# A two-layer decoder trunk on one core: the output product reads sums that the DMA queues have added up, with four smaller edits in the attention layers

## The chip, the cores and the metric

The kernel runs on one core of a Trainium2 chip. The metric is the device time of one execution in microseconds (us), as the median of several runs. The core's engines work side by side, each on its own instructions in their written order: TensorE (PE) multiplies matrices, VectorE (DVE) and ScalarE (ACT) do elementwise work, GpSimd (POOL) a little of it, and SyncE (SP) issues most of the DMA transfers. POOL can issue DMAs too, from a queue of its own. An engine that waits for one instruction waits with everything behind it.

## The reference, cut to what matters

Two layers on a sequence of 1024 rows of 1024 elements, all in float32. Each layer has an attention, a residual with LayerNorm, a gated feed-forward (ff) and another residual with LayerNorm.

```python
ALPHA = (2 * DEPTH) ** 0.25
for i in range(2):
    y = diff_attention(h, ...) if i == 0 else forgetting_attention(h, ...)
    h = layer_norm(ALPHA * h + y, ln1_g[i], ln1_b[i])
    f = conv_ffn(h, ...)
    h = layer_norm(ALPHA * h + f, ln2_g[i], ln2_b[i])

def conv_ffn(x, w_in, conv_w, conv_b, w_out):       # D_FF = 2816
    gate, up = split(x @ w_in, 2)
    gate = causal_conv_width_3(gate, conv_w) + conv_b
    return (silu(gate) * up) @ w_out
```

The differential attention of layer 0 has 8 pairs of heads. For a pair, one softmax minus lambda times another multiplies the values, and each 128-wide row of the result `o` is divided by its root mean square (`rms_norm`). The forgetting attention of layer 1 has 16 heads; a forget gate per head and row (`f_logit = x @ w_f`, 16 columns) adds a running sum to the scores.

## The kernel before

**Precision.** A float32 operand is kept as two float32r parts, `hi` (a rounded copy, made on ACT, line 89) and `lo` (the rest, a subtraction on DVE, line 91). This is `split`. A product is three matmuls, `mm3` (lines 100 to 102): hi by hi, lo by hi, hi by lo, all added up in one PSUM bank. A plain float32 matmul is shown as two passes (x2 in the timeline).

**Order of the work.** Layer 0's attention, its output projection and norm, its ff up product, its ff output product, and then the same for layer 1. In the attention, the tiles of the next pair's projections (`m<-xh,wh`) fill PE between the scores, the transposes (line 1371) and the value products. Jobs are Python generators. `tick` starts the work of a job and `tock` ends it, and what is written earlier in these functions stands earlier in each engine's queue. Tiles come from named pools with a fixed number of buffers, and an engine waits where the pool has no free one. The framework's scheduler decides the last detail of the order from this.

**Places that the change touches.**
- `scores` (lines 519 to 535): a strip of scores of ln = 128 (qt+1) columns is cut at 512; each part is one matmul with the hi part of the keys (line 533) and one with the lo part (line 534). For ln = 640 the parts have 512 and 128 columns. This happens 32 times, 16 in each layer.
- `diff_values` (lines 597 to 613): the block norm of layer 0. A matmul of all ones with the squares gives every partition the sum over the 128 (line 606, plain float32), and ACT and DVE turn it into the norm's factor. Each of the 8 pairs has two groups of 512 query rows (the last pair three groups).
- `gate_logits` (lines 618 to 636): the forget gates' logits, by `mm3` with 16-wide weights, for 8 blocks of the contraction and 2 halves of the rows, so 48 matmuls.
- `Values.evacuate` (called in `tick`, line 787): copies transposed probabilities out of PSUM as their hi and lo parts, `pt<-m`.
- `gated` (lines 1115 to 1134): for each of the 22 blocks f of the ff's inner dimension, the convolution, silu and two multiplies; the tile is stored to DRAM, `ad[f]`.
- `down_steps` (lines 1144 to 1326): the output product, (1024 x 2816) by (2816 x 1024), by one level of a Strassen-Winograd scheme: 7 products m of quarter operands in place of 8. Each has k = 0..10 blocks of the contraction and j = 0..3 blocks of rows, three matmuls each, so one step (m, k) is 12 matmuls of 512 columns. The passes are ((1,2), (6,5), (7,3), (4,)). For each k, `load_a` and `load_b` fetch quarters of the left operand (from `ad`) and of the weight, `sub` (line 1198) forms the scheme's sums and differences on DVE, `make` splits them into `oa` and `wo`, and `drain` (line 1267) adds a finished bank to the accumulator `acc`. `when(i, ...)` ties a load or a sum to a step, LEAD = 10 steps before its use. `Ffn.run` calls the makes up to AHEAD = 6 steps in advance.
- `Norm` (`stats`, `root`, `apply`, lines 1476 to 1515) for the LayerNorm. In the last pass (m = 4) each row block j is drained, normed and, in layer 1, stored.

Of the kernel before, what the change touches and what calls it, by code (L numbers as in the profile page):

```python
# [48 lines left out]
S2, S3 = 1, 1  # L49
M7, G4 = 15, 5  # L50
# [6 lines left out]
class Trunk:  # L57
# [64 lines left out]
    def consts(self):  # L122
# [14 lines left out]
        self.ones = cp.tile([P, P], F32, name="ones")  # L137
        nc.vector.memset(self.ones, 1.0)
# [381 lines left out]
    def scores(self, q, kd, kl, h, qt, l):  # L520
# [76 lines left out]
    def diff_values(self, of, ob, q0, q1):  # L597
# [3 lines left out]
        rd = self.tp.tile([P, 512], F32, tag="sq", name=self.nm("sq"), bufs=1)[:, :w]  # L601
        nc.scalar.activation(rd, osl, AF.Square)
# [3 lines left out]
        nc.tensor.matmul(ms, self.ones, rd, start=True, stop=True)  # L606
# [3 lines left out]
        nc.vector.scalar_tensor_tensor(ms, ms, P * RMS_EPS, rd, op0=ALU.add, op1=ALU.mult)  # L610
        nc.vector.scalar_tensor_tensor(osl, osl, self.gsub, rd, op0=ALU.mult, op1=ALU.mult)
        nc.vector.tensor_tensor(ms, ms, rd, op=ALU.mult)
# [5 lines left out]
    def gate_logits(self, c):  # L618
        nc = self.nc
        if c == 0:  # L620
            st = self.tmp()[:, :P]
            nc.sync.dma_start(st, self.i["wf"])
            self.wf = [self.cp.tile([P, 128], F32R, name=f"wf{j}") for j in range(2)]
            self.split(*self.wf, st)
# [7 lines left out]
        for kt in range(KT):  # L632
            ws = slice(16 * kt, 16 * kt + 16)
            self.mm3(ps[:16], self.wf[0][:, ws], self.wf[1][:, ws], self.xh[kt, c], self.xl[kt, c],
                     kt == 0, kt == KT - 1)
        nc.vector.tensor_scalar(self.z[:16, c * 512:c * 512 + 512], ps[:16], self.bf, None, op0=ALU.add)

    def forget_gates(self):
# [19 lines left out]
        nc.vector.tensor_tensor_scan(c, self.ones, l, 0.0, op0=ALU.mult, op1=ALU.add)  # L658
# [118 lines left out]
    def tick(self, live, values, job):  # L777
# [8 lines left out]
        for v in values:  # L786
            v.evacuate()
# [18 lines left out]
    def tock(self, values):  # L806

        n = 1 if values and values[0].l == 0 else 2
        for v in values:
            n -= v.turn(n)  # L810
        for v in values:
# [303 lines left out]
    def gated(self, l, f, d):  # L1115
# [16 lines left out]
        nc.vector.tensor_tensor(t[:, :512], t[:, :512], d["b"][:, 512:], op=ALU.mult)  # L1132
        nc.vector.tensor_tensor(t[:, 512:], t[:, 512:], d["b"][:, :512], op=ALU.mult)
        nc.sync.dma_start(self.ad[f], t)

# [8 lines left out]
    def down_steps(self, l):  # L1144
# [3 lines left out]
        self.norm2 = None  # L1148
# [15 lines left out]
        def load_a(k, *blocks):  # L1164

            nonlocal n_h
            for r in blocks:
                if r == 22 or (r, k) == (21, H - 1):
                    if n_h % 2 == 0:
                        self.half = self.qp.tile([P, 1024], F32, tag=f"q{1 - self.own}", name=self.nm("ha"))  # L1170
# [417 lines left out]
```

## Time and profile before

| | |
|---|---|
| median of 3 runs | 2470.56 us (2469.18 to 2472.64) |
| profiled execution | 2472.59 us, of it the span 2470.8 us |
| granted TensorE clock | 0.994 of full speed |
| PE busy | 2421.0 us (98%), 11377 matmuls |
| DVE busy | 1893.9 us (77%) |
| ACT busy | 1239.2 us (50%) |
| POOL busy | 141.2 us (6%) |
| DMA | 266.02 MB, mean 108 GB/s |

The profile shows one execution. A group of instructions gives the busy time, the mean duration and the idle time that stood ahead of it with what ended that idle time. Matmuls are pipelined, and the end of each is modelled, so a row of 0.39 us and the next row's start overlap: what one matmul costs is the distance between two starts. A bracket behind a row of a timeline is the idle time before it and its releaser.

The stages in the span: layer 0's attention to about 443 us, its projection and norm to 590, the up product to 988, the output product to 1160, layer 1's projections and gates to 1275, its attention to 1700, and its second output product from about 2240 to 2460.

### The profile page before, as it was taken

Reading aid. Unit: us, or ns where it says so; the run is one execution under the profiler, and the core shown is the slowest. Engines: PE = TensorE matmul, PEld = TensorE weight load, DVE = VectorE, ACT = ScalarE, POOL = GpSimd, SP = SyncE. Lnnn points to the kernel's source line nnn. Section 1 sums busy time; section 2 is a strip of 40 time slices with the busy share of each in tenths; the row PEclk is TensorE's granted clock in tenths of the full one; section 3 lists DMA queues with packets and bytes.
Section 4 is the critical chain, followed back from the end, with each engine's and each line's share of the span. In section 5 each row is a group of like instructions: output and inputs, shape, how many; then the busy total and the mean of one; then the engine's idle time right before and its main releaser. Section 6 shows DMA issues by size and latency. Waiting matters only on the chain. (4 is left out here: it accounts for less than half of the span.)

```text
span 2470.8 us, 32550 instructions
## 1 busy us (share of the span) xinstructions
PE 2421.0 (98%) x11377; PEld 1984.9 (80%) x11377; DVE 1893.9 (77%) x3588; ACT 1239.2 (50%) x2311; POOL 141.2 (6%) x323
## 2 busy tenths in 40 slices
PE   9999999999999999989999999999999999999998
PEld 7887778778888888878778888888878888888776
DVE  5887877989767667696857777778888666666978
ACT  4555556556544444434545555555465444445344
POOL 2111111010000000000100000000010000000000
PEclk9999999999999999999999999999999999999999
DMA  6223223532322224842422222224223222228622
GB/s 182 65 84 91 81 82 92 174 110 80 103 77 77 95 85 140 298 157 74 138 70 73 65 65 65 65 81 155 94 79 101 77 89 90 77 85 301 206 86 98
DMA packets 111940, 266.02 MB, mean 108 GB/s; under 512 B 17648, under 2 KB 24816, under 8 KB 111776
## 3 DMA queue, kind: packets, MB, share of 16 engines
q1 hardware_dynamic: 110816, 262.83, 33.4%
q8 instruction: 90, 1.47, 0.2%
q0 software_dynamic: 672, 1.05, 0.2%
q14 instruction: 74, 0.61, 0.1%
q10 hardware_dynamic: 288, 0.07, 0.0%
HBM read 182.68 MB, written 47.64 MB: 93 GB/s over the span
## 5 line engine op out<-in xcount | busy, mean ns | idle before, releaser
L100 PE MATMUL m<-xh,wh 128*128 128x512 f32 x768 | 320.3, 417 | 7.0 <-DVE pt L91 6.6
L101 PE MATMUL m<-xl,wh 128*128 128x512 f32 x768 | 302.7, 394 | 1.7 <-DVE xl L91 1.7
L102 PE MATMUL m<-xh,wl 128*128 128x512 f32 x768 | 302.8, 395 | 0.0
L100 PE MATMUL m<-xh,wo 128*128 128x512 f32 x656 | 255.4, 389 | 0.0
L102 PE MATMUL m<-xh,wo 128*128 128x512 f32 x656 | 255.3, 389 | 0.0
L101 PE MATMUL m<-xl,wo 128*128 128x512 f32 x656 | 255.2, 389 | 0.0
L89 ACT ACTIVATE pt<-m 128x512 fp32r<-128x512 f32 (+3 forms) x285 | 137.6, 492 | 182.8 <-PE m L1371 120.6
L540 DVE CUSTOM_DVE_ANT_0 s<-s,mask 128x384 f32<-128x384 f32 (+7 forms) x256 | 194.5, 760 | 42.4 <-PE s L534 41.5
L89 ACT ACTIVATE wo<-wg 128x512 fp32r<-128x512 f32 x168 | 106.5, 634 | 225.0 <-PE m L102 218.4
L100 PE MATMUL m<-q,wo 128*128 128x512 f32 x472 | 184.1, 390 | 0.0
L91 DVE TENSOR_TENSOR pt<-m,pt 128x512 fp32r<-128x512 f32 (+3 forms) x285 | 156.7, 558 | 35.6 <-ACT pt L89 31.7
L101 PE MATMUL m<-q,wo 128*128 128x512 f32 x472 | 183.8, 389 | 0.0
L102 PE MATMUL m<-q,wo 128*128 128x512 f32 x472 | 183.7, 389 | 0.0
L100 PEld LDWEIGHTS m<-xh,wh 128*128 128x128 f32 x768 | 145.7, 190 | 38.3 <-DVE pt L91 11.2
L102 PEld LDWEIGHTS m<-xh,wl 128*128 128x128 f32 x768 | 145.0, 189 | 31.3 <-DVE wl L91 0.2
L101 PEld LDWEIGHTS m<-xl,wh 128*128 128x128 f32 x768 | 145.5, 190 | 27.5 <-issue 2.9
L89 ACT ACTIVATE wo<-t 128x512 fp32r<-128x512 f32 x132 | 82.8, 627 | 145.3 <-PE m L102 133.2
L91 DVE TENSOR_TENSOR wo<-wg,wo 128x512 fp32r<-128x512 f32 x168 | 115.3, 687 | 41.1 <-ACT wo L89 40.2
L527 POOL CAST qz<-q 64x128 fp32r<-64x128 f32 x256 | 96.6, 378 | 845.1 <-PE s L534 773.2
L100 PEld LDWEIGHTS m<-xh,wo 128*128 128x128 f32 x656 | 123.1, 188 | 26.0 <-ACT pt L1093 0.6
L101 PEld LDWEIGHTS m<-xl,wo 128*128 128x128 f32 x656 | 123.1, 188 | 25.7
L102 PEld LDWEIGHTS m<-xh,wo 128*128 128x128 f32 x656 | 123.1, 188 | 25.6 <-DVE wo L91 0.2
(341 smaller groups left out, 5875.6 us busy)
## 6 DMA issues: line engine op xcount, KB each, us to landing
wst<-in_w SPq DMA_DIRECT2D x46, 512.0 KB, 3.9
t<-in_wi SPq DMA_DIRECT2D x44, 512.0 KB, 4.5
ad<-t SPq DMA_DIRECT2D x44, 512.0 KB, 3.7
ha<-ad SPq DMA_DIRECT2D x88, 256.0 KB, 5.5
wg<-in_wi SPq DMA_DIRECT2D x42, 512.0 KB, 3.5
wb<-in_wd SPq DMA_DIRECT2D x84, 256.0 KB, 3.2
q<-q SPq DMA_DIRECT2D x128, 128.0 KB, 2.2
pt<-in_wd SPq DMA_DIRECT2D x48, 256.0 KB, 4.5
```

The costliest lines, as they stand in the source:

```text
L89: nc.scalar.activation(hi, src, AF.Copy, scale=1.0 if scale is None else scale)
L91: nc.vector.tensor_tensor(lo, src, hi.bitcast(F32), op=ALU.subtract)
L100: mm(out, wh, xh, start=start, stop=False)
L101: mm(out, wh, xl, start=False, stop=False)
L102: mm(out, wl, xh, start=False, stop=stop)
L527: nc.gpsimd.tensor_copy(qz[r:r + 64, :], q[r:r + 64, qt * P:qt * P + P])
L540: self.nc.vector.tensor_tensor_reduce(sb[:, :ln], sb[:, :ln], self.mask[:, 1024 - ln:], 1.0, BIG, ALU.add, ALU.min, mn)
```

## The change

1. `scores`: ln = 640 is cut into two parts of 320 columns.
2. `diff_values`: for the first seven pairs the squares are split into hi and lo (tiles `hl`), and the sum is two float32r matmuls with ones. ACT gets a copy and a Square, DVE a subtraction for the split and one multiply less. The result goes to a tile of the pool "lg". The last pair keeps the plain float32 sum.
3. `gate_logits`: hi and lo parts of the weights stand in one 48-wide tile (hi, 16 zeros, lo), so one matmul with the hi part of the rows gives both sums, and one more matmul adds hi by lo. A DVE add joins them.
4. `evacuate` for layer 1 moves from the next `tick` to the end of `tock`, one tick sooner.
5. `gated` negates the first product, adds the two halves of the tile (`e`, a DVE add per f) and stores three more strips for f = 0..10 (`sd` 6, 7 and 3). For f = 11..21 POOL issues three DMAs that add to what lies in DRAM: the tile's second half onto `ad[k]` and `sd["6"][k]`, and `e` onto `sd["3"][k]`. Those of the last two f are issued in steps 9 and 12 of the output product.
6. The output product reads the left operand of each product as one strip from DRAM (`ad` or `sd`), 7 per k where it was 4, and forms no sums of left operands. Weight sums stay. The drains subtract. The strips come from the pools of `xh` and `xl`. The last pass takes three single k and then a group of 8 (before 6 and 5), its row blocks in the order 0, 2, 1, 3, and the first norm halves are applied one step sooner. A step makes at least all of its own operands.

The core of the diff (S3, G4, ORDER and the drains' signs are left out where they only follow):

```diff
-S2, S3 = 1, 1
-M7, G4 = 15, 5
+S2, S3 = 1, 0
+M7, G4 = 15, 8
+ORDER = (0, 2, 1, 3)
...
-        for c in range((ln + 511) // 512):
-            ks = slice(c * 512, min(ln, c * 512 + 512))
+        w = ln // 2 if ln == 640 else 512
+        sb = sb[:, 512 - w:512 - w + ln]
+        for c in range(0, ln, w):
+            ks = slice(c, min(ln, c + w))
...
+            hl = self.lp.tile([P, 1024], F32R, tag="lg", name=self.nm("hl"))
+            h, l = hl[:, :w], hl[:, 512:512 + w]
+            self.split(h, l, sq)
...
+            nc.tensor.matmul(ms, self.ones, h, start=True, stop=False)
+            nc.tensor.matmul(ms, self.ones, l, start=False, stop=True)
...
-            self.mm3(ps[:16], self.wf[0][:, ws], self.wf[1][:, ws], self.xh[kt, c], self.xl[kt, c],
-                     kt == 0, kt == KT - 1)
+            both = self.wf[:, kt], self.xh[kt, c]
+            high = self.wf[:, kt, :16], self.xl[kt, c]
+            for i, (w, x) in enumerate((both, high) if kt == 0 else (high, both)):
+                nc.tensor.matmul(ps[:w.shape[1]], w, x, start=kt + i == 0, stop=kt == KT - 1 and i == 1)
...
         for v in values:
-            v.evacuate()
+            if v.l == 0:
+                v.evacuate()
...
+        nc.vector.tensor_tensor(e, t[:, :512], t[:, 512:], op=ALU.add)
+        def adds():
+            for out, x in ((self.ad[k][:, 512:], t[:, 512:]), (self.sd["6"][k], t[:, 512:]), (self.sd["3"][k], e)):
+                nc.gpsimd.dma_start(out, x, accum_op=ALU.add)
+        if f == k:
+            for r in ("6", "7", "3"):
+                nc.sync.dma_start(self.sd[r][k], e)
...
-            sub(a[21, k], a[21, k], a[22, k], ALU.add)
...
+            a[m, k] = strip("ha")
+            nc.sync.dma_start(a[m, k], self.sd[str(m)][k] if m in (3, 6, 7) else
+                              self.ad[k + (0 if m in (1, 5) else H)][:, lo if m < 3 else hi])
...
-            if m == 6:
-                x = sub(a[21, k], a[21, k], a[11, k])
-                return x, sub(a[11, k], b[22, k], b[12, k])
+            if m == 6:
+                return minus(b[11, k], b[12, k], b[22, k])
...
-            self.make(n)
+            self.make(max(n, (self.first + [len(self.makes)])[i + 1]) if i >= self.up else n)
```

**Order, layer 0's attention.** DVE's queue in the second group of a pair, about 128 to 136 us of the span. `pt` is a part of the transposed probabilities, `wl` the lo part of a weight, `m` and `s` PSUM banks, `of` the pair's output, `rs` a row's factor. Before:

```order
L91 TENSOR_TENSOR q_1061<-t_1085,q_1059 128x512
L540 ISA s_1474,nm_1479<-s_1474,mask 128x896
L540 ISA nm_1479 128x1
L91 TENSOR_TENSOR wl_1606<-wst_1523,wh_1605 128x1024
L91 TENSOR_TENSOR pt_1542<-m_1493,pt_1542 128x128
L610 SCALAR_TENSOR_TENSOR m_1495<-m_1495,sq_1409 128x512
L611 SCALAR_TENSOR_TENSOR of_998<-of_998,gsub,sq_1409 128x512
```

The same place now:

```order
L543 ISA s_1515,nm_1520<-s_1515,mask 128x896
L543 ISA nm_1520 128x1
L92 TENSOR_TENSOR q_1097<-t_1123,q_1095 128x512
L92 TENSOR_TENSOR pt_1585<-m_1534,pt_1585 128x128
L584 RECIPROCAL rs_1634<-ls_1522 128x1
L586 TENSOR_SCALAR p_1592<-p_1592,rs_1634 128x896
L624 SCALAR_TENSOR_TENSOR of_1031<-of_1031,gsub,rd_1539 128x512
L625 SCALAR_TENSOR_TENSOR m_1536<-m_1536,sq_1447 128x512
L543 ISA s_1574,nm_1579<-s_1574,mask 128x896
L543 ISA nm_1579 128x1
L626 SCALAR_TENSOR_TENSOR of_1031<-m_1536,of_1031 128x512
L92 TENSOR_TENSOR wl_1652<-wst_1566,wh_1651 128x1024
```

The last part of the probabilities, `pt` of 128 columns, stood behind the weight's subtraction and now stands eight instructions ahead of it.

**Order, layer 0's output product.** DVE's queue at the end of its first pass, about 1047 to 1056 us. `ha` and `wb` are strips of the operands, `oa` and `wo` their parts for PE, `acc` the accumulator, `s` and `m` its banks in PSUM. Before:

```order
L1198 TENSOR_TENSOR ha_9009<-ha_9009,ha_9390 128x512
L1198 TENSOR_TENSOR ha_9496<-ha_9496,ha_9098 128x512
L1267 SCALAR_TENSOR_TENSOR acc_9346<-acc_9346,s_9247 128x512
L1267 SCALAR_TENSOR_TENSOR acc_9347<-acc_9347,s_9247 128x512
L1198 TENSOR_TENSOR ha_9098<-wb_9592,pt_9594 128x512
L1198 TENSOR_TENSOR pt_9839<-pt_9839 128x512
L1267 SCALAR_TENSOR_TENSOR acc_9348<-acc_9348,s_9248 128x512
L91 TENSOR_TENSOR wo_9722<-wb_9547,wo_9722 128x512
L91 TENSOR_TENSOR oa_9730<-ha_9443,oa_9730 128x512
L91 TENSOR_TENSOR wo_9729<-ha_9049,wo_9729 128x512
L1267 SCALAR_TENSOR_TENSOR acc_9346,sums_9401<-acc_9346,m_9280 128x512
L1267 SCALAR_TENSOR_TENSOR acc_9347,sums_9401<-acc_9347,m_9281 128x512
```

The same place now:

```order
L1226 TENSOR_TENSOR wb_9960<-wb_9412,wb_9960 128x512
L1230 SCALAR_TENSOR_TENSOR wb_9412<-wb_9960,wb_9962 128x512
L1293 SCALAR_TENSOR_TENSOR acc_9540<-acc_9540,s_9438 128x512
L1293 SCALAR_TENSOR_TENSOR acc_9541<-acc_9541,s_9438 128x512
L92 TENSOR_TENSOR wo_9914<-wb_9737,wo_9914 128x512
L1293 SCALAR_TENSOR_TENSOR acc_9542<-acc_9542,s_9439 128x512
L92 TENSOR_TENSOR oa_9922<-ha_9733,oa_9922 128x512
L92 TENSOR_TENSOR wo_9921<-wb_9247,wo_9921 128x512
L1293 SCALAR_TENSOR_TENSOR acc_9540,sums_9592<-acc_9540,m_9475 128x512
L1293 SCALAR_TENSOR_TENSOR acc_9541,sums_9592<-acc_9541,m_9476 128x512
```

The sums of `ha` with `ha` are gone, and two fewer instructions stand between the first drain and the first drain of an `m` bank. The drains' own order is as it was.

**Order, layer 1's attention.** DVE's queue early in the attention; the ISA rows are the mask and row minimum of the scores (`s`). Before:

```order
L91 TENSOR_TENSOR pt_12319<-m_12290,pt_12319 128x512
L540 ISA s_12309,nm_12312<-s_12309,mask 128x384
L540 ISA nm_12312 128x1
L91 TENSOR_TENSOR pt_12322<-m_12295,pt_12322 128x384
L697 RECIPROCAL rs_12360<-ls_12274 128x1
L698 TENSOR_SCALAR wh_12363<-wh_12363,rs_12396 128x384
```

The same place now:

```order
L92 TENSOR_TENSOR pt_12536<-m_12527,pt_12536 128x512
L92 TENSOR_TENSOR pt_12539<-m_12532,pt_12539 128x384
L543 ISA s_12553,nm_12556<-s_12553,mask 128x384
L543 ISA nm_12556 128x1
L714 RECIPROCAL rs_12630<-ls_12558 128x1
L715 TENSOR_SCALAR wh_12603<-wh_12603,rs_12630 128x384
```

Both parts of the probabilities now stand ahead of the next scores' mask; before, the second stood behind it.

## Rows read from the trace of the kernel before

**Rows 1.** The page's first part: busy time, share of the span and instructions of each engine.

```profile
PE 2421.0 (98%) x11377; PEld 1984.9 (80%) x11377; DVE 1893.9 (77%) x3588; ACT 1239.2 (50%) x2311; POOL 141.2 (6%) x323
```

**Rows 2.** The list of waits of PE over the whole span: what waited, for what, us in total, times, the longest.

```profile
PE m L100 <- DVE pt L91: 7.1, 7, 1.7
PE s L100 <- DVE acc L1267: 6.5, 3, 3.3
...
PE s L100 <- ACT wo L89: 3.7, 2, 1.9
...
PE s L101 <- DVE wo L91: 1.3, 2, 0.7
PE m L1371 <- DVE q L91: 1.1, 6, 0.2
```

**Rows 3.** The timeline of PE around one block norm of layer 0: start, duration, engine, line, operation, idle before.

```profile
129.75 1.02 PE L606 MATMUL m<-sq,ones 128*128 128x512 f32 x2
...
130.84 0.39 PE L101 MATMUL m<-xl,wh 128*128 128x512 f32 x1
...
132.23 0.39 PE L101 MATMUL m<-xl,wh 128*128 128x512 f32 x1
132.46 0.39 PE L102 MATMUL m<-xh,wl 128*128 128x512 f32 x1
133.80 0.50 PE L100 MATMUL m<-xh,wh 128*128 128x512 f32 x1 [0.95 <-DVE pt L91]
```

**Rows 4.** The timelines of DVE (first two) and ACT (the last) over the same 3 us.

```profile
132.32 1.23 DVE L91 TENSOR_TENSOR wl<-wst,wh 128x1024 fp32r<-128x1024 f32 x1 [1.15 <-ACT wh L89]
133.46 0.28 DVE L91 TENSOR_TENSOR pt<-m,pt 128x128 fp32r<-128x128 f32 x1
...
132.76 0.27 ACT L89 ACTIVATE pt<-m 128x128 fp32r<-128x128 f32 x1
```

**Rows 5.** The timeline of PE over one strip of 640 scores.

```profile
112.91 0.39 PE L533 MATMUL s<-q,q 128*128 128x512 f32 x1
...
113.38 0.22 PE L533 MATMUL s<-q,q 128*128 128x128 f32 x1
...
113.55 0.39 PE L100 MATMUL m<-pt,q 128*128 128x384 f32 x1
```

**Rows 6.** The groups of PE from 1170 to 1300 us, shapes apart: the first of the three of the gate logits (the others have the same count and 6.3 us each).

```profile
L100 PE MATMUL m<-xh,wf 128*16 128x512 f32 x16 | 6.4, 399 | 0.0
```

**Rows 7.** Busy time by stretch: length, then PE, PEld, DVE, ACT and POOL with counts, then the granted clock, the share of the DMA engines and GB/s. The stretches are layer 0's up product and three parts of its output product.

```profile
590.00:988.00 398.00, 397.49 (x1753) 328.29 (x1752) 287.68 (x402) 188.53 (x290) 0.00 (x0) 1.00 0.29 95
988.00:1041.00 53.00, 53.00 (x236) 43.88 (x235) 35.44 (x55) 24.83 (x41) 0.00 (x0) 1.00 0.86 301
1041.00:1098.00 57.00, 52.95 (x232) 43.18 (x231) 53.21 (x93) 21.13 (x36) 0.00 (x0) 1.00 0.56 184
1098.00:1160.00 62.00, 59.42 (x254) 48.44 (x254) 48.07 (x78) 25.58 (x45) 0.00 (x0) 0.97 0.27 85
```

**Rows 8.** The timeline of PE in the two output products: the waits there.

```profile
1055.28 0.50 PE L100 MATMUL s<-wo,oa 128*128 128x512 f32 x1 [3.25 <-DVE acc L1267]
...
1106.94 0.50 PE L100 MATMUL s<-wo,oa 128*128 128x512 f32 x1 [1.94 <-ACT wo L89]
1108.09 0.53 PE L101 MATMUL s<-wo,oa 128*128 128x512 f32 x1 [0.64 <-DVE wo L91]
...
2306.09 0.50 PE L100 MATMUL s<-wo,oa 128*128 128x512 f32 x1 [2.91 <-DVE acc L1267]
```

**Rows 9.** The timeline of DVE ahead of the first of these waits.

```profile
1049.72 0.68 DVE L1198 TENSOR_TENSOR ha<-wb,pt 128x512 f32<-128x512 f32 x1
...
1050.92 0.68 DVE L1267 SCALAR_TENSOR_TENSOR acc<-acc,s 128x512 f32<-128x512 f32 x1
...
1054.54 0.68 DVE L1267 SCALAR_TENSOR_TENSOR acc<-acc,s 128x512 f32<-128x512 f32 x1
```

**Rows 10.** The groups of DVE from 990 to 1170 us: the sums of the left operand.

```profile
L1198 DVE TENSOR_TENSOR ha<-ha,ha 128x512 f32<-128x512 f32 x42 | 27.6, 685 | 9.4 <-DMA ha<-ad 9.3
```

**Rows 11.** DMA issues, first of the page (SP's queue, the whole span), then of the first 40 us (POOL's queue): count, KB each, median us from issue to landing.

```profile
ha<-ad SPq DMA_DIRECT2D x88, 256.0 KB, 5.5
...
rope<-rope POOLq DMA_DIRECT2D x2, 256.0 KB, 3.7
```

**Rows 12.** The timeline of PE in layer 1's attention: one group of four transposes and the start of the next.

```profile
1386.01 0.44 PE L1371 MATMUL m<-ident,p 128*128 128x128 f32 x2
1386.28 0.27 PE L1371 MATMUL m<-ident,t 128*128 128x128 f32 x1
1386.39 0.27 PE L1371 MATMUL m<-ident,p 128*128 128x128 f32 x1
1386.85 0.41 PE L1371 MATMUL m<-ident,p 128*128 128x128 f32 x2 [0.19 <-DVE q L91]
```

**Rows 13.** The timeline of the end: PE's last matmul, and DVE's drain and last step of the norm for an earlier row block (first two of DVE) and for the last (last of DVE).

```profile
2459.64 0.39 PE L102 MATMUL s<-wo,oa 128*128 128x512 f32 x1
...
2452.16 0.69 DVE L1267 SCALAR_TENSOR_TENSOR acc<-acc,s 128x512 f32<-128x512 f32 x1 [0.98 <-PE s L102]
...
2455.95 1.28 DVE L1515 SCALAR_TENSOR_TENSOR acc<-pt,n,lg 128x1024 f32<-128x1024 f32 x1
...
2465.88 1.41 DVE L1515 SCALAR_TENSOR_TENSOR p<-pt,n,lg 128x512 f32<-128x512 f32 x2
```

More of the change, by code (lines that the diff above doesn't have):

```diff
@@ L600, in diff_values @@
         nc.scalar.copy(osl, ob[:, :w])
-        rd = self.tp.tile([P, 512], F32, tag="sq", name=self.nm("sq"), bufs=1)[:, :w]
-        nc.scalar.activation(rd, osl, AF.Square)
+        sq = self.tp.tile([P, 512], F32, tag="sq", name=self.nm("sq"), bufs=1)[:, :w]
+        nc.scalar.activation(sq, osl, AF.Square)
+        last = p == NP - 1
+        if not last:
+            hl = self.lp.tile([P, 1024], F32R, tag="lg", name=self.nm("hl"))
+            h, l = hl[:, :w], hl[:, 512:512 + w]
+            self.split(h, l, sq)
         for _ in range(1 + FL):
@@ L622, in gate_logits @@
             nc.sync.dma_start(st, self.i["wf"])
-            self.wf = [self.cp.tile([P, 128], F32R, name=f"wf{j}") for j in range(2)]
-            self.split(*self.wf, st)
+            self.wf = self.tt.tile([P, 1024], F32R, tag="pt", name="wf")[:, :48 * KT].rearrange("p (k n) -> p k n", k=KT)
+            nc.gpsimd.memset(self.wf[:, :, 16:32].bitcast(F32), 0.0)
+            self.split(self.wf[:, :, :16], self.wf[:, :, 32:], st.rearrange("p (k n) -> p k n", k=KT))
             self.bf = self.cp.tile([16, 1], F32, name="bf")
@@ L810, in tock @@
             n -= v.turn(n)
+        for v in values:
+            if v.l:
+                v.evacuate()
         for v in values:
@@ L1249, in product @@
                     banks[m] = [self.mbank() for _ in range(4)]
-            for j in range(4):
+            for n, j in enumerate(ORDER if m == 4 else range(4)):
                 js = slice(j * P, j * P + P)
-                jl = slice(512 + j * P, 512 + j * P + P)
                 for k in ks:
                     x, w = ops[m, k]
-                    self.mm3(banks[m][j], x[:, js], x[:, jl], w[:, lo], w[:, hi],
-                             k == 0 and not more, k == H - 1, more)
+                    self.mm3(banks[m][j], *[t[:, js] for t in x], *w, k == 0 and not more, k == H - 1, more)
                 if ks[-1] == H - 1 and (j or m == 4):
@@ L1316, in down_steps @@
             when(11 + tt if tt < 4 else 20 + tt, half, tt, int(tt > 3))
[L1317 removed]
+            when((30 if tt < 4 else 44) + tt, half, tt, int(tt < 4))
         def norm():
@@ L1322, in down_steps @@
         when(6, norm)
+        for j in range(2):
+            when(9 + 3 * j, lambda j=j: self.late_adds[j]())
         m6 = len(steps) - (H + 1 - G4)
@@ L1334, in run @@
         self.ad = [self.dr.tile([P, 1024], F32, name=f"ad{f}") for f in range(NF)]
+        self.sd = {r: [self.dr.tile([P, 512], F32, name=f"sd{r}{k}") for k in range(NF // 2)] for r in "673"}
         self.resid = self.i["x"].rearrange("(t p) d -> t p d", p=P)
```

136 lines of the change are left out of this document (68 added, 68 removed).

## The prediction

> **What bounds the kernel now.** I read the page's first part first. PE is busy for 98% of the span [rows 1], so a change gains only by giving PE fewer or shorter matmuls, by taking away a time in which PE stands, or at the two ends. I then took the list of PE's waits [rows 2] to see what the standing costs, the windows by stage [rows 7] to see which engine is near its limit where, and the timelines around each wait [rows 3, 4, 8, 9]. The reader is to see two things. A normal matmul of 512 columns takes 0.23 us from start to start (132.23 to 132.46 in [rows 3]). And in layer 0's output product DVE, elsewhere with room, is busy for 53.2 of 57 us [rows 7], and there the longest waits of PE stand, for a drain and for `wo` [rows 8].
>
> **The change part by part.** All terms are against the profiled execution, 2472.59 us (span 2470.8). It lies 2.0 us above the median of 2470.56, so I take them from the median as they are.
>
> *Block norm.* The two passes of the float32 sum and one normal matmul take from 129.75 to 130.84, 1.09 us [rows 3]. Two float32r matmuls and a normal one take 3 x 0.23 = 0.69. There are 14 such groups (7 pairs by 2), so 14 x 0.40 = 5.6 us. The added copy and Square on ACT and the split on DVE are covered: over the span ACT is busy for 50% and DVE for 77% [rows 1]. The factor is used a good while later, by the output projection. Without that cover each would cost at most the 0.6 or so that a 512-wide DVE step takes (50.92 against 49.72, two such steps, [rows 9]), 14 times.
>
> *Scores of 640.* Two parts of 512 take 112.91 to 113.38, 0.47 us, and two of 128 take 0.17 [rows 5], together 0.64. Four of 320, by columns, take 4 x 0.235 x 320/512 = 0.59. That is 0.05 x 32 = 1.6 us. Nothing shows 320 columns; between 0 and 3 us.
>
> *Gate logits.* A third of the 48 matmuls goes [rows 6], 16 x 0.23 = 3.7 us. The other sums gain a small DVE add, twice.
>
> *Six stalls in layer 0.* PE waits seven times for `pt` [rows 2], 7.1 us; six of them come once per pair, as at 133.80, where 1.34 us pass since 132.46 in place of 0.23. So one costs 1.1 us, six cost 6.6. The cause is a queue: DVE's last part of `pt` (128 columns, 0.28 us) stood behind the weight's subtraction of 1.23 us, which started at 132.32 because it had waited for ACT; ACT's copy of `pt` at 132.76 came behind that too [rows 4]. In the changed order `pt` stands eight instructions ahead of that subtraction on DVE. Next to be late is the weight itself, which a later tile needs; I take 6.0, with 0 as the one end (ACT's two added instructions make `pt`'s copy as late as it was) and 7.5 as the other.
>
> *Output product.* The waits there are 6.5 for drains, 3.7 and 1.3 for `wo`, 11.5 us over both layers [rows 2]; the two kinds recur at the same places in layer 1 [rows 8]. After one, the clock stands at its half level (1.2 GHz): the granted clock of the stretch from 1098 is 0.97 over 62 us [rows 7], 1.9 us, and layer 1 has a like one after the wait at 2306, so 3.8 more. Together 15.3 us. They come from DVE: it forms 42 sums of left operands in layer 0's part alone, 27.6 us [rows 10], and before the wait at 1055.28 [rows 8] it worked without a break through sums, splits and drains until the drain at 1054.54 that released PE [rows 9]. These sums go; per k DVE has 6 instructions in place of 8 in the second pass, 5 for 7 in the third and 4 for 5 in the first. In the stretch of 57 us, ten k's of it, that is about 20 x 0.6 = 12 us off 53.2, so DVE is no longer the limit. The drains' own order stays, with splits and two `m` drains between the third and the fourth, so a late DVE would still stall PE: the gain hangs on DVE's arriving in time, not on the order. I take 14, with ends of 3 (only the instructions missing ahead of that drain, about 0.6 at each, and less of the rest) and 16. Loads: four per k in the first pass in place of six, where the DMA engines now stand at 0.86 and 301 GB/s [rows 7], and four in the next where they stand at 0.56. A transfer from `ad` lands after 5.5 us [rows 11] and is issued ten steps of 2.7 us ahead, so it is covered; without the cover a late strip holds up DVE and all behind it.
>
> *Adds in DRAM.* In the up product one f takes 398 us x 84/1753 = 19.1 us [rows 7] (84 matmuls per f). For f = 0..10 SP issues three stores more, which wait for `e`, 0.6 us of DVE behind the tile whose store SP waits for anyway; the loads behind them are ahead of need. DVE's 22 adds, 13 us, lie in 110 us of room (287.7 of 398). For f = 11..21 POOL issues three adding DMAs per f; POOL has no other work in that stretch [rows 7]. The trace has no adding DMA. A plain one of the same size on POOL's queue lands after 3.7 us [rows 11]; on SP's queue 5.5. Three in a row would be 11 to 16.5 us, below 19.1, even if one waits for the other, so I cost them at nothing.
>
> The Trainium skill, "Collectives: The Full Stack" (section "The bandwidth ceiling: the fold count and why AG ≠ RS ≠ AR"), speaks against that: an add in the DMA engine needs two source reads and runs at about half of a copy's rate. No run here shows one yet; by this rule an add would be 2 x 3.7 = 7.4 us (an estimate from rows 11 and that page), and three of them 22.2.
>
> *Layer 1's sooner split.* Four transposes take from 1386.01 to 1386.85, though two neighbours start 0.11 apart [rows 12]: 0.84 against 0.44. The wait list has six of 1.1 us together, and the pace shows 0.4 at each of a dozen places, 5 us. Sooner splits free the banks sooner, but they also stand ahead of the next scores' mask. I take 3, between 5 gained and 5 lost.
>
> *The tail.* The last drain and norm ends at 2467.3, 7.3 us behind PE's last matmul (2460.0); an earlier row block needs 5.1 from its drain (2452.16) to the end of its step (2457.2), and the last one queues behind the one before [rows 13]. With 8 k's of three matmuls, 5.5 us per row block in place of 3.4, it no longer does: 2 us, between 0 and 3.
>
> *New waits.* Seven strips per k wait in pools that the up product leaves one after the other, and I allow one wait as long as the one at 1055 [rows 8]: 3 us, between 0 and 15.
>
> Sum: 5.6 + 1.6 + 3.7 + 6.0 + 14 + 3 + 2 - 3 = 32.9 us. 2470.6 - 33 = 2437.6 us, about 2437.
>
> **The rivals.**
> A. The output product keeps its waits. For it: DVE's order is fixed, so one strip that lands late holds the queue, and the strips of the left operand need three loads more per k. Against it: DMA share falls where it was highest. 2437 + 14 = 2451.
>
> B. The adding DMAs are slower than an f. Place: the last eleven f of the up product, in both layers. If one takes 8 us and they follow each other, three take 24, 4.9 us more than an f, and 11 f's fall behind by 54. One f of 19 us is hidden by the spare buffers of the tile `t`, so each layer loses some 35 us, both 70: 2437 + 70 = 2507. It beats the gain of 33 from (33/2 + 19)/11 = 3.2 us per f, 7.4 us for one add. For it: nothing in the trace shows an add. Against it: 3.7 us for a copy, and 16 DMA engines at a share of 0.29 in that stretch [rows 7], which can have several in flight.
>
> The price of the skill's rule above is 7.4 us, right at that point: about 2470, no change.
>
> C. The attention gives back what the single edits save. For it: the splits of layer 1 stand ahead of the masks that the next scores wait for, ACT has two instructions more per group in layer 0, and both attentions have many small waits, which move when an order moves. Against it: no listed wait there but the six is over 2 us. The six stalls stay (+6) and layer 1 loses 3 in place of gaining 3 (+6): 2449.
>
> D. Every wait that goes is replaced by one of the same length (A and C at once), and only the matmul terms come, 5.6 + 1.6 + 3.7 = 10.9 us: 2460. For it: the clock and the waits follow the order as a whole. Against it: DVE has less to do in just the stage where it is at 93% [rows 7].
>
> **How the numbers follow.** Forecast 0.57, A 0.14, C 0.12, D 0.06, B 0.07, adds just at an f's length 0.04. The likeliest is 2437. Its own range, from the terms' ends, is 2424 to 2450; with A and C and part of their spread it is 2424 to 2456, which leaves D, B and half of the margins out. 0.2% is 5 us, about what a measurement of this kernel can tell from no change. Faster: 0.57 + 0.14 + 0.12 + 0.06 = 0.89; same 0.04; slower 0.07.
>
> **What would show it.** In the profile of the changed kernel: 14 pairs of float32r sums 0.23 us apart; 32 gate matmuls; no wait of about 1 us for `pt` once per pair in layer 0; the waits for drains and `wo` gone from the list, and the clock at 1.00 from 1098 on; DVE below 80% in the second pass; POOL's adds landing well below 6.4 us each; the last DVE step some 5 us behind the last matmul. The prediction is wrong if PE waits in the up product for tiles that an add still reads, if a strip's DMA releases DVE in the output product, or if the waits in layer 1 grow.

## The result, and the profile after

The changed kernel takes 2453.03 us (median of 4 runs, 2450.94 to 2454.11), the kernel before beside it 2469.87 us: a ratio of 0.9931, with a 95% interval of 0.9917 to 0.9945. That is 16.8 us faster, half of the 33 us that were forecast, and inside the stated range. The profiled execution has a span of 2451.3 us against 2470.8.

PE's list of waits, as in [rows 2]: what waited, for what, us in total, times, the longest.

```profile
PE s L101 <- DVE acc L1293: 9.2, 4, 3.4
...
PE m L504 <- ACT t L459: 3.8, 4, 1.2
PE m L101 <- DVE pt L1116: 3.6, 2, 1.8
PE m L101 <- ACT pt L1114: 1.7, 2, 1.3
...
PE m L101 <- DVE pt L92: 0.7, 2, 0.5
```

The waits for `wo` of [rows 2] (3.7 and 1.3 us) are gone, and so are the six for `pt`, of which 0.7 us are left. But the wait for a drain has grown from 6.5 to 9.2 us, and two waits are new: L1114 and L1116 copy and add up the up product's last banks, and PE waits for these copies. The timeline of PE shows where these waits stand in layer 0 (layer 1 has the same four):

```profile
970.44 0.50 PE L101 MATMUL m<-xh,wo 128*128 128x512 f32 x1 [1.31 <-ACT pt L1114]
...
980.69 0.50 PE L101 MATMUL m<-q,wo 128*128 128x512 f32 x1 [1.79 <-DVE pt L1116]
...
1046.68 0.47 PE L101 MATMUL s<-wo,oa 128*128 128x512 f32 x1 [1.52 <-DVE acc L1293]
...
1050.81 0.79 PE L101 MATMUL s<-wo,oa 128*128 128x512 f32 x1 [2.50 <-DVE acc L1293]
```

The stretches that answer to [rows 7] (length, busy times of PE, PEld, DVE, ACT and POOL, granted clock, share of the DMA engines, GB/s), the up product first, then the three parts of the output product:

```profile
576.00:975.80 399.80, 397.98 (x1753) 328.34 (x1752) 299.40 (x421) 187.53 (x289) 26.81 (x30) 1.00 0.47 130
987.00:1045.00 58.00, 58.00 (x257) 47.85 (x255) 33.22 (x54) 25.01 (x44) 2.90 (x4) 1.00 0.90 296
1045.00:1098.00 53.00, 48.98 (x209) 40.00 (x209) 38.71 (x67) 20.86 (x38) 0.00 (x0) 0.97 0.63 199
1098.00:1160.00 62.00, 62.00 (x275) 51.36 (x274) 45.58 (x74) 28.88 (x52) 0.00 (x0) 1.00 0.58 184
```

DVE is relieved as forecast: 38.7 of 53 us (73%) in the second pass, where it was at 93%. Yet PE waits at that pass's start, and the clock is at 0.97 there. The DMA engines have not been relieved: 0.90 in the first pass, 0.86 before.

What holds the drains up is on DVE's timeline ahead of them (compare [rows 9], where DVE worked without a break):

```profile
1043.92 0.69 DVE L1226 TENSOR_TENSOR wb<-wb,wb 128x512 f32<-128x512 f32 x1 [7.47 <-DMA wb<-in_wd]
1044.64 0.69 DVE L1230 SCALAR_TENSOR_TENSOR wb<-wb,wb 128x512 f32<-128x512 f32 x1
1045.26 1.28 DVE L1293 SCALAR_TENSOR_TENSOR acc<-acc,s 128x512 f32<-128x512 f32 x2
...
1050.07 0.68 DVE L1293 SCALAR_TENSOR_TENSOR acc<-acc,s 128x512 f32<-128x512 f32 x1
```

DVE stood for 7.5 us on a weight sum whose strip had not landed, and the drains that PE was waiting for stood behind it in the queue. At the end of the up product ACT stands in the same way for strips of the left operand, with the copy of a bank (L1114) behind them:

```profile
969.29 0.63 ACT L90 ACTIVATE oa<-ha 128x512 fp32r<-128x512 f32 x1 [2.72 <-DMA ha<-ad]
969.82 0.57 ACT L1114 COPY pt<-m 128x512 f32<-128x512 f32 x1
```

So most of what the output products were to gain was lost to late strips. A table by stage shows it. The boundaries are matmuls that both traces have: the first score, the first `m<-xh,wo` of an up product and the first matmul of an output product (46.3, 586.9, 990.7, 1238.2, 1838.3 and 2241.8 before; 46.3, 576.0, 984.7, 1227.5, 1819.5 and 2225.4 after). A difference below zero is a gain.

| stage | before | after | difference |
|---|---|---|---|
| layer 0 attention (first score to the first `m<-xh,wo` of the up product) | 540.6 | 529.7 | -10.9 |
| layer 0 up product (from there to its end) | 403.7 | 408.7 | +5.0 |
| layer 0 output product, and layer 1 to its first score | 247.5 | 242.8 | -4.7 |
| layer 1 attention | 600.1 | 592.1 | -8.1 |
| layer 1 up product | 403.5 | 405.9 | +2.4 |
| layer 1 output product and end | 229.0 | 225.9 | -3.1 |

The third row holds 1.8 us of the gate matmuls' gain (8 of the 16 matmuls; the rest is in the fourth) and the last one 2.2 of the tail. So the two output products are faster by 2.9 and 0.9 us in themselves, where 14 us had been forecast, and the two up products lose 7.4 at their ends: together a loss of 3.6. Layer 0's output product runs from 990.7 to 1214 us in the trace before, so the three parts in [rows 7] are its first 170 us and not the whole.

### The profile page after: what moved, and what is told of

It reads as the page before. It is cut to its first block, busy times and chain, and to the rows that moved or that the text cites. A ratio compares the mean times of both kernels' runs of the same rounds, so it can differ in the third digit from the quotient of the medians.

```text
span 2451.3 us, 33031 instructions
## 1 busy us (share of the span) xinstructions
PE 2404.3 (98%) x11361; PEld 1982.9 (81%) x11361; DVE 1869.8 (76%) x3543; ACT 1245.4 (51%) x2342; POOL 198.8 (8%) x390
## 3 DMA queue, kind: packets, MB, share of 16 engines
q0 software_dynamic: 10176, 18.36, 4.6%
## 5 line engine op out<-in xcount | busy, mean ns | idle before, releaser
L101 PE MATMUL m<-xh,wh 128*128 128x512 f32 x768 | 314.2, 409 | 0.3 <-ACT xh L90 0.3
L90 ACT ACTIVATE pt<-m 128x512 fp32r<-128x512 f32 (+3 forms) x285 | 131.3, 491 | 115.2 <-PE m L1401 111.2
L536 PE MATMUL s<-q,q 128*128 128x512 f32 (+4 forms) x384 | 132.4, 347 | 2.1 <-ACT wst L581 1.3
```

Source lines behind the costliest of these rows:

```text
L90: nc.scalar.activation(hi, src, AF.Copy, scale=1.0 if scale is None else scale)
L101: mm(out, wh, xh, start=start, stop=False)
```

## The experiments

The theories: (1) the attention part earns the whole gain and the output product part gives some back; within that, (1a) the adding DMAs take the DMA engines' time and make strips late, or (1b) DVE's queue order does it, weight sums ahead of drains, with loads late for want of free strips. The rivals stand in the expectations. The runs were made in three groups, on chips on which the kernel before took 2469.9, 2466.5 and 2467.1 us, so ratios are compared between groups: 0.001 is 2.5 us.

**The two halves of the change, each alone.** `small_edits` has the first four parts on the kernel before, `product_only` the last two.

```diff
+        for c in range(0, ln, w):
...
+            self.split(h, l, sq)
...
+            both = self.wf[:, kt], self.xh[kt, c]
...
+            if v.l == 0:
+                v.evacuate()
```

```diff
+M7, G4 = 15, 8
...
+                nc.gpsimd.dma_start(out, x, accum_op=ALU.add)
...
+            a[m, k] = strip("ha")
```

> The attention edits alone (halved strips of 640, float32r block norm, stacked gate weights, sooner split), with the output product of the kernel before. Theory 1 (the output product part costs time, the attention part earns all of the gain): by stages of the two traces the attentions and the gates gained 10.9 + 3.8 + 8.1 = 22.8 us, so 2470 - 23 = 2447 us, faster than the full change. Theory 2 (the output product part earns its share, and the attention's gain came partly with it): 2458 us or more.

> The output product part alone (adds by DMA, strips from DRAM, order of the last pass), with the attention of the kernel before. Theory 1: the waits that go (for wo, 3 + 1.6 us a layer with the clock) come back as waits for drains and at the end of the up product, so 2470 + 3 = 2473 us. Theory 2: 2462 us or less.

Measured: 2455.08 us for the small edits (ratio 0.9945, 0.9926 to 0.9963) and 2473.53 us for the product part (1.0012, 1.0002 to 1.0022). The product part alone cost 3.7 us, as theory 1 had it; its interval just leaves out no change. The small edits earned 14.8 us, less than the 23 expected; that sum had counted the half of the gates' gain that falls into layer 1's attention twice, so 21 was due. 2455 lies between the bounds of the two theories. The two ratios multiply to 0.9957 against 0.9931 for the full change, hardly more than the intervals allow. A part of this difference can be seen: PE's waits of the small edits from 1100 to 1235 us, of which the full change has only the third.

```profile
PE s L535 <- DMA q<-q: 2.3, 1, 2.3
PE m L102 <- DVE n L1507: 1.3, 1, 1.3
PE m L503 <- ACT t L458: 0.7, 1, 0.7
```

The full change thus lacks 3.6 us of waits that the small edits alone meet at layer 1's start. The granted clock tells of more: in the small edits it stands at its half level once in layer 0's attention and twice in layer 1's (0.83 each from 425 to 435, 1225 to 1235 and 1778 to 1788 us, 1.7 us lost at each), in the full change not at all in these stages. Which line of the full change takes these away was not tried. Theory 1's claim stands for the product part by itself: it costs time.

**The full change without its adding DMAs.**

```diff
-                nc.gpsimd.dma_start(out, x, accum_op=ALU.add)
+                pass
```

> The full change with the adding DMAs left out (the sums over the two halves of the inner dimension are missing from the output). Theory 1a (the adds take the DMA engines' time, so that strips and weights land late): the waits of PE at the end of the up product (3.4 us and a stretch at half clock in layer 0, 2.5 in layer 1) and the waits for drains (4.3 and 5.8 us, each with a stretch at half clock) go or shrink to a third: 2453 - 12 = 2441 us. Theory 1b (DVE's queue order: weight sums stand ahead of the drains, and their loads are late because SP waits for free strips): only the waits at the end of the up product go, 2453 - 5 = 2448 us, and the drains' waits stay within 1 us.

Measured: 2436.02 us (0.9862, 0.9843 to 0.9880), 17 us below the full change (0.9931). Both kinds of waits went, in both layers. What is left of PE's waits from 960 to 1170 us:

```profile
PE s L103 <- DVE oa L92: 1.4, 1, 1.4
PE s L101 <- DVE acc L1293: 0.5, 1, 0.5
```

That is 1a and more: 0.9862 x 2470.56 is 2436.5 us, beside a forecast of 2437.6. A kernel that leaves work out can win by the missing work, though, so this needed the next ones.

**Weight sums held behind the drains.**

```diff
+        drained = []
...
+        def held():
+            return self.tc.issue_after(drained[-1]) if drained else ExitStack()
...
         def sub(dst, x, y):
-            nc.vector.tensor_tensor(dst, x, y, op=ALU.subtract)
+            with held():
+                nc.vector.tensor_tensor(dst, x, y, op=ALU.subtract)
             return dst
...
+            drained.append(getattr(ins, "ins", ins))
```

> The full change, with each weight sum of the output product held on DVE behind the drain that the program issued last before it. Theory 1b: the waits for drains (4.3 us in layer 0, 5.8 in layer 1, and 1.5 to 2 us each at half clock) go, 2453 - 12 = 2441 us, and the waits at the end of the up product stay. Theory 1a: the splits wait for the same late strips, so 2453 - 3 = 2450 us at best.

Measured: 2459.9 us (0.9963, 0.9951 to 0.9975), 7 us slower than the full change. The gain of theory 1b did not come, and the 2450 of 1a was missed too. The weight sums do stand behind the drains now, and DVE stands at the same place for something else that is late. Its timeline:

```profile
1038.00 0.29 DVE L92 TENSOR_TENSOR wf<-t,wf 128x128 fp32r<-128x128 f32 x1 [7.13 <-ACT wf L90]
...
1043.41 0.69 DVE L92 TENSOR_TENSOR q<-ha,q 128x512 fp32r<-128x512 f32 x1 [2.40 <-ACT q L90]
1044.02 0.68 DVE L1300 SCALAR_TENSOR_TENSOR acc<-acc,s 128x512 f32<-128x512 f32 x1
```

The waits of 7.1 and 2.4 us took the place of the 7.5, the drain came at 1044.0, and new waits stood elsewhere (one of 4.7 us for `wo` in layer 1's output product). In this run the split of the gate weights `wf` also came to stand ahead of the drain (1038.0, in the full change at 1060.6), behind a copy on ACT that had waited 7.6 us for their load. So this is no clean test of the order alone: the order changed which late load was waited for first, and loads stayed late. The run `paired` below, with the order of the full change, settles 1b.

**The bytes, or the adding.** Each add replaced by a plain store of the same bytes; the sums are missing.

```diff
-                nc.gpsimd.dma_start(out, x, accum_op=ALU.add)
+                nc.gpsimd.dma_start(out, x)
```

> The full change with each adding DMA replaced by a plain store of the same bytes on the same queue (the sums are missing from the output). Theory 1a-read (an add takes twice the time of the DMA engines): the share of POOL's queue falls to about half and a good part of the 17 us comes back, 2444 us or less. Rival (POOL's queue as such, or the order of stores and loads, whatever the DMAs do): 2453 us.

Measured: 2437.53 us (0.9887, 0.9870 to 0.9905). By the ratios 11 of the 17 us came back (0.9931 to 0.9887, without any add 0.9862), with every byte still written by the same queue. The intervals of the stores and of no adds (0.9843 to 0.9880) overlap, so whether the stores themselves cost the other 6 us is open. The waits at the end of the up product went but for 0.3 us; drains were still waited for, 4.5 us in layer 0. POOL's queue on the two pages (packets, MB, share of 16 engines), first the full change, then the stores:

```profile
q0 software_dynamic: 10176, 18.36, 4.6%
```

```profile
q0 software_dynamic: 5952, 18.36, 2.0%
```

Without the 0.2% that this queue has in every kernel, 66 adds take 4.4% of 2451 us, 1.63 us of all sixteen engines each, and 66 stores 1.8% of 2433, 0.66 us, by the time of their packets: an add takes 2.5 times a store. In the up product alone (600 to 960 us, 27 of them) the queue has 12.7% against 4.9%, which is 1.69 and 0.65 us. From issue to landing, from 960 to 1045 us, the full change (first fence) and the stores (second):

```profile
ha<-ad SPq DMA_DIRECT2D x32, 256.0 KB, 8.9
...
sd<-t POOLq DMA_DIRECT2D x4, 256.0 KB, 9.8
ad<-t POOLq DMA_DIRECT2D x2, 256.0 KB, 7.0
```

```profile
ha<-ad SPq DMA_DIRECT2D x31, 256.0 KB, 6.2
...
sd<-t POOLq DMA_DIRECT2D x4, 256.0 KB, 5.9
ad<-t POOLq DMA_DIRECT2D x2, 256.0 KB, 5.3
```

By these medians strips on SP's queue landed 2.7 us later beside the adds than beside the stores, but each trace tells the landing of only three of them: 8.9, 8.9 and 6.6 us against 6.2, 5.5 and 6.8. The two of 8.9 were issued at 972 and 998 us, while three adds each were under way (966 to 978, 993 to 1005).

**Which of the adds.** Only the six of f = 20 and 21 in each layer left out; their part of the sums is missing.

```diff
-            self.late_adds.append(adds)
+            self.late_adds.append(lambda: None)
```

> The full change without the adding DMAs of f = 20 and 21 alone (six per layer, issued in the first pass of the output product; their part of the sums is missing from the output). If these six hold up the first pass: the drains' waits go (6 us in layer 0, 8 in layer 1, with the clock), the waits at the end of the up product stay, 2440 us. If the adds of f = 18 and 19, which meet the first strips at the end of the up product, set the delay for all that follows: both stay, 2450 us.

Measured: 2432.99 us (0.9862, 0.9848 to 0.9877). The ratio is the same as without any add. Within the intervals these six of each layer were the whole cost, and the other 27 cost nothing that can be measured. From 960 to 1170 us PE waited for:

```profile
PE m L101 <- ACT pt L1114: 1.1, 1, 1.1
PE m L101 <- DVE acc L1293: 0.6, 1, 0.6
```

I had expected the waits at the end of the up product to stay, since the six are written into steps 9 and 12 of the output product. They went. POOL's timeline of the full change shows why:

```profile
946.96 0.86 POOL L1163 DMA_DIRECT2D ad<-t  x1 [16.39 <-DVE wo L92]
...
966.00 0.88 POOL L1163 DMA_DIRECT2D ad<-t  x1 [16.37 <-DVE wo L92]
966.59 2.07 POOL L1163 DMA_DIRECT2D sd<-t  x2
993.17 0.89 POOL L1163 DMA_DIRECT2D ad<-t  x1 [24.50 <-DVE t L1155]
```

Steps 9 and 12 start at 1009.6 and 1017.8 us in this trace. But POOL's queue holds nothing else there, so the adds of f = 20 and 21 go as soon as their tile is done, at 966 and 993: with the first strips at the end of the up product, and in the first pass.

DVE's stand of 7.5 us ends at 1043.9, 39 us after the last of these adds has landed (1004.9). SP's queue shows the link. It issues the same 170 loads of layer 0's output product in the same order in both runs. Ahead of the first three adds the full change is 0.7 us early, behind them 3.8 us late, behind the second three 6.6 to 7.8 us, and it does not make this up in that pass. One weight strip shortly before the stand, in the full change and without the six:

```profile
1036.23 0.33 SPq L1217 DMA_DIRECT2D wb<-in_wd  x1
```

```profile
1029.80 0.33 SPq L1217 DMA_DIRECT2D wb<-in_wd  x1
```

So the six adds put the whole queue of loads back, and PE pays where a late load meets a drain. What SP waits for at each of these loads, room in its queue or a free strip, was not separated.

**The six adds really held.** They go behind a small copy that waits for the first drain. The gate weights' staging tile `st` gets a place of its own in this run.

```diff
-            st = self.tmp()[:, :P]
+            st = self.small(P, "st", bufs=1)
...
-        for j in range(2):
-            when(9 + 3 * j, lambda j=j: self.late_adds[j]())
+        def held():
+            mark = self.small(tag="hold", bufs=1)
+            ins = nc.gpsimd.tensor_copy(mark, acc[0][:, :1])
+            with self.tc.issue_after(getattr(ins, "ins", ins)):
+                for fn in self.late_adds:
+                    fn()
...
+        when(20, held)
```

> The full change with the six adding DMAs of f = 20 and 21 held on POOL's queue behind a small copy that waits for the first accumulator's drain (about 1045 us in layer 0), in place of going as soon as their tile is done; the gate weights' staging tile has a place of its own, so that it doesn't wait for the tiles that are held. If it is the place of these six adds, beside the first strips and weights, that costs: as without them, 2434 to 2441 us, with no drain wait over 1 us. If six adds cost the same wherever they stand in the output product's first half, or the held tiles make new waits: 2448 us or more.

Measured: 2436.98 us (0.9885, 0.9868 to 0.9901), with the whole computation. POOL's timeline:

```profile
1038.70 0.18 POOL L1352 COPY hold<-acc 128x1 f32<-128x1 f32 x1 [50.38 <-DVE acc L1293]
1039.28 0.87 POOL L1163 DMA_DIRECT2D ad<-t  x1 [0.40 <-DMA wb<-in_wd]
```

From 960 to 1170 PE waited 1.3 us in all. Layer 1 kept one wait of 2.4 us for a drain. The expectation of no drain wait over 1 us thus missed there, and the time held. The tiles that these adds read stay taken 46 to 73 us longer than in the full change, so it was not the holding of the tiles that cost.

**The sums on DVE.** The blocks are worked in pairs k, k + 11, and DVE forms the three sums before they are stored.

```diff
+        f = f // 2 + f % 2 * (NF // 2)
...
+        tt(t0[:, 512:], t0[:, 512:], t[:, 512:])
+        nc.sync.dma_start(self.ad[k][:, 512:], t0[:, 512:])
+        tt(g[:, 512:], e0[:, :512], t[:, 512:])
+        nc.sync.dma_start(self.sd["6"][k], g[:, 512:])
+        tt(g[:, :512], t[:, :512], g[:, 512:])
+        nc.sync.dma_start(self.sd["3"][k], g[:, :512])
```

> The full change, but the 22 blocks f are worked in pairs k, k + 11, so that the three sums per k are made on DVE in the up product (three more DVE adds of 0.6 us per k, in a stage where DVE has room) and stored once; no adding DMA is left, and the strips, the loads and the output product are those of the full change. Theory 1a (the adding DMAs are what delays strips and weights): as without the adds, 2436 to 2441 us, and no wait of PE over 1 us at the end of the up product and at the drains. Rival 3 (any added traffic of that size just ahead of the output product does it): the last pair's five stores stand in the same place, so the waits at the end of the up product stay, and it is 2446 us or more.

Measured: 2435.45 us (0.9871, 0.9855 to 0.9887), 31 us below the kernel before beside it, with the whole computation; by the ratios 15 us below the full change. The last pair's six stores in the same place did no harm, so rival 3 falls as the main cause. They are fewer bytes than the stores and adds of the full change at that place, so they do not settle the 6 us that the run with plain stores left open. DVE's order is that of the full change, weight sums ahead of the drains, and the first of these sums waits 1.4 us for its strip where it had waited 7.5. So 1b falls with this run. The up product took the added DVE work without a wait:

```profile
577.00:974.30 397.30, 397.30 (x1753) 328.42 (x1752) 311.11 (x442) 187.48 (x289) 0.00 (x0) 1.00 0.32 111
```

DVE is at 311 of 397 us there, PE has no idle time, and the DMA share is 0.32 against 0.47. In the first pass (987 to 1045 us) the share is 0.90, as in the full change, and no wait of PE over 1 us comes of it: the share alone does not say whether strips are late. This version and `late_held` both beat the change as it was made.

**Single parts of the attention.** The kernel before with the sooner split alone, and with the float32r block norm alone; one execution of each.

```diff
+            if v.l == 0:
+                v.evacuate()
```

```diff
+            nc.tensor.matmul(ms, self.ones, h, start=True, stop=False)
+            nc.tensor.matmul(ms, self.ones, l, start=False, stop=True)
```

> The kernel before with the sooner split in layer 1 alone. If it earns what layer 1's attention gained in the full change, that stretch (first score to first matmul of the up product) is 600.1 - 7 = 593 us or less; if the halves and the order after them earned it, 598 us or more.

> The kernel before with the float32r block norm alone. If the fewer passes (14 x 0.4 = 5.6 us) and the six waits for the last part of the probabilities (6.6 us) both go by this edit, layer 0's attention up to the first matmul of the up product takes 586.9 - 11 = 576 us or less; if the waits' going hung on something else, 581 us.

With the sooner split layer 1's attention took 593.7 us, 6.4 less than before:

```profile
1234.15:1827.85 593.70, 589.48 (x3077) 487.90 (x3076) 455.99 (x1030) 319.68 (x691) 52.85 (x138) 1.00 0.27 83
```

It misses the bound of 593 by 0.7 and is far from 598: most of the 8.1 us of that stage came with the split. With the block norm alone, the up product's first `m<-xh,wo` came at 579.2 us, between the two bounds (576 and 581). The six waits for `pt` did go, but others came; PE's waits from 88 to 443 us:

```profile
PE m L503 <- ACT t L458: 2.1, 2, 1.1
PE s L533 <- ACT wst L578: 1.3, 1, 1.3
PE m L1381 <- DVE of L623: 1.2, 5, 0.3
```

## Why the prediction was right in its sign and half of its size

**Block norm, scores, gates.** Near the forecast. In the trace before, each of the 14 groups has a matmul 0.41 us late behind the plain float32 sum; none is left. The four matmuls of the strip of 640 shown here take 0.58 us (114.05 to 114.63) in place of 0.64; over all 32 strips they take 0.60 on the mean, 1.2 us in all, forecast 1.6.

```profile
114.05 0.30 PE L536 MATMUL s<-q,q 128*128 128x320 f32 x1
114.19 0.31 PE L537 MATMUL s<-q,qz 128*128 128x320 f32 x1
...
114.63 0.28 PE L101 MATMUL m<-pt,q 128*128 128x256 f32 x1
```

The gate logits have 32 matmuls; a 48-wide one takes no longer than a 16-wide one in [rows 6], so the 3.7 us are there.

```profile
L650 PE MATMUL m<-xh,wf 128*48 128x512 f32 x16 | 6.4, 398 | 0.0
L650 PE MATMUL m<-xl,wf 128*16 128x512 f32 x16 | 6.0, 392 | 0.0
```

**Six stalls in layer 0.** These waits went, and the gain did not come. The six waits of [rows 2] left 0.7 us. But in the stage of the table's first row all of PE's waits add up to 15.2 us before and 14.0 after. What comes late next was the transposes' and the norm's inputs, not the weight that I named: the waits for `t` at line 504 come to 3.2 us there (three of the four in the list above), and five short ones for `of`, as in the run with the block norm alone, to 1.2. So this term was worth 1.2 us where I had put 6.0.

That the stage still gained 10.9 us, near the 5.6 + 6.0 + 0.8 = 12.4 that were forecast, is luck. Before, the clock stood at its half level twice in this stage, which no term had counted:

```profile
90.00:100.00 10.00, 8.44 (x39) 6.59 (x38) 9.47 (x23) 6.73 (x15) 1.88 (x3) 0.83 0.35 79
440.00:450.00 10.00, 8.49 (x38) 6.79 (x39) 7.55 (x22) 2.70 (x8) 0.29 (x1) 0.83 1.01 372
```

Each cost 1.7 us (0.17 of 10), and the full change has none there. The three traces with the old norm have two such stretches in this stage, those with the new one have one or none; which wait decides it was not tried.

**Layer 1's sooner split.** Right in sign and near in size. Alone it took 6.4 us off the stage, of which 1.7 are again a stretch at the half clock (0.83 from 1795 to 1805 us before, none in that run). The 4.7 left lie inside the stated end of 5; the forecast was 3. [rows 12] show 0.4 us at one place; I had counted a dozen such places.

**The tail.** Right. PE's last matmul and DVE's last step:

```profile
2442.72 0.39 PE L103 MATMUL s<-oa,oa 128*128 128x512 f32 x1
...
2446.78 1.41 DVE L1545 SCALAR_TENSOR_TENSOR p<-pt,n,lg 128x512 f32<-128x512 f32 x2
```

2448.2 - 2443.1 = 5.1 us in place of 7.3.

**Adds in DRAM: the step that failed.** "Three in a row would be 11 to 16.5 us, below 19.1, even if one waits for the other, so I cost them at nothing." The queue did keep up: the three adds of f = 20 are issued from 966.0 on and have landed at 978.5, 12.5 us later, and without the adds of f = 11 to 19 as well the time is the same as without the last six alone. The prices were too low, though: the 3.7 us of [rows 11] belong to a load, and on that queue a plain store landed after 5.6 us in the median (4.5 to 7.3) and an add after 8.1 (6.3 to 11.3). The error was to ask only whether the queue keeps up with an f, and to ask it only of the up product. The last six run beside the first strips and weights, at the place where I had read a share of 0.86 myself [rows 7], each takes the DMA engines for 2.5 times a store's time, and SP's loads fall 7 to 8 us behind. Their price was not the 0 of the sum but, by the ratios, 17 us without them (0.9862), 11 with them held (0.9885) and 15 with the sums on DVE (0.9871), against the full change's 0.9931. That is about the far end, 15, of what I had allowed for new waits, or beyond it. Signs of being wrong that I had named came too: a strip's DMA released DVE in the output product, and the adds did not land well below 6.4 us.

By the Trainium skill, "Collectives: The Full Stack" (section "The bandwidth ceiling: the fold count and why AG ≠ RS ≠ AR"), the add of a ring's ReduceScatter needs two source reads, so that it runs at about half of AllGather's rate. For a kernel's own adding DMAs the runs here show 2.5 times a store, so the direction agrees; the second read itself is not shown, both queues have 18.36 MB. I had weighed the rule as a matter of one f's length, where it gave 2470, and that did not come: the adds of an f overlap.

**Output product.** With the six adds out of the way the 14 us came: by the boundaries of the table, and without the gates and the tail, the two output products of the paired version are about 8 us faster each than before. A few us of that are uncertain, since the two traces come from chips on which the kernel before differs by 3.4 us. The mechanism (DVE's sums gone, waits for drains and `wo` gone with them) was right. The total, 0.9871 x 2470.56 = 2438.7 us against a forecast of 2437.6, is nearer than its terms are: the six stalls gave far less than their 6.0. As the change was made, it was rival A that happened, with 2451 against 2453.0 measured: "one strip that lands late holds the queue". That A's time is so near is partly luck, since it too counted 6.0 us for the six stalls. A's reason was off in part. I had put it down to three strips more per k; the strips are the same in `paired`, and there they do no harm. Against A I had said that the DMA share falls where it was highest; it rose from 0.86 to 0.90, but `paired` has 0.90 there as well.

**Rivals B, C, D.** B did not happen: PE's clock and waits in the up product up to 960 us stay as they were. C happened in layer 0 for the waits, where 4.8 of the 6.0 us did not come and the clock hid it; layer 1 went the other way. D's 2460 did not come: the output product did exchange its waits for others of about the same length, at the up product's end too, but the attentions and the tail kept their gains.

## What to carry to other kernels

Price a new DMA at the place where it will run, by the loads of other queues that stand there, and look up in the order of its queue when that is: a transfer on an otherwise empty queue goes when its data are ready, whatever step it is written into. In an engine's in-order queue one late load holds up everything behind it, so a transfer that is off the critical path can still cost PE time. Where an engine has room in the stage before, three small adds on it can be cheaper than an add in DRAM. And when a stage's time agrees with its terms, add up its waits and its granted clock as well: here one term's gap was filled by another that nobody had written down.

## What the runs showed of the hardware that was not expected

An accumulating DMA of 256 KB took 1.63 us of all sixteen DMA engines, a plain store of the same bytes 0.66, a ratio of 2.5, as shares of packet time in these kernels. The clock fell to its half level after waits of 1.52 and 2.50 us within 4 us (at 1050.81: the matmuls behind it are 0.43 us apart, the stretch stands at 0.97), while a wait of 3.25 us before did not lower it ([rows 8], at 1055.28: the stretch of [rows 7] is at 1.00 there). With the stores in place of the adds, waits of 0.74, 2.50 and 1.30 us at the same drains left it at 1.00 (1030 to 1060 us), and in the kernel before one wait of 1.94 us (to 1796.55) was followed by a fall. The length of the one wait alone does not say whether the clock falls; what does was not tried.
